# A two-layer decoder trunk: block products of the expert down projection, seven for eight in 38 of 64 steps

## The chip, the cores and the metric

The kernel runs on one core of one Trainium2 chip. The metric is the device time of one execution in microseconds (us). Three runs of the kernel before gave 3980.77, 3981.47 and 3985.25 us; the median is 3981.47.

Names: PE is TensorE (matrix products), PEld its weight loads, DVE is VectorE, ACT ScalarE, POOL GpSimd, SP the queue that issues DMAs. [...] "L356" is line 356 of the kernel file.

## The reference

Two layers. In each, 512 tokens of width 1024 pass a mixer (four parallel heads), then PEER, an expert layer with a product-key choice of 16 of 16384 one-neuron experts for each of 8 heads, then a gated embedding.

```python
def peer(z, w_q, sub_keys, u_tab, v_tab):
    ...
    def block(args):
        zt, et, gt = args
        act = jax.nn.gelu(jnp.einsum('tkd,td->tk', u_tab[et], zt))
        return jnp.einsum('tk,tkd->td', gt * act, v_tab[et])
...
        h = h + peer(rmsnorm(h, ffn_norm[l]), peer_wq[l], peer_subkeys[l], peer_u[l], peer_v[l])
```

The kernel does not gather. It computes the activations of all 16384 experts, multiplies them by a gate that is zero where an expert was not chosen, and multiplies the result (512 x 16384) by V (16384 x 1024).

## The kernel before

The experts are cut into 128 chunks of 128. All products are f32r matrix products of 128 x 128 weights with 512 columns. Each factor is split into a high part (a copy rounded by ACT, L359) and a low part (the difference, on DVE or POOL, L360), and a product is three matrix products: high by high, high by low, low by high (`group3`).

For a chunk the up product is 24 matrix products into one bank `ps_u` (`u_mm`), then ACT's gelu into `dact`. `weigh` multiplies by the gates `dg` on DVE (L341) and splits into `whi`, `wlo`; `split_v` splits the chunk of V into `vhi`, `vlo` (128x1024). The down product works on two chunks at a time: `down(a0, dh)` makes, for one half of the 1024 output columns, four token blocks of 128 tokens; each is six matrix products into a bank `ps_v` and one DVE addition to the residual `h` (L1695).

One pass of the final loop of `gen_dense` (L1735) is one chunk: loads for later chunks, `split_v` and `up` of the chunk two ahead, then four token blocks of `down`. The up products of the first 60 chunks (`NA`) have been made earlier, in `gen_ahead`, beside the choice of the experts and the gates, and went to DRAM (`Ad`); they are loaded again. The up products of the other 68 chunks are made in the loop.

So the expert stage of a layer has two stretches: chunks 0 to 59, in which PE has only down products and DVE all the small work, and chunks 60 to 127, in which up and down products alternate and POOL makes `ulo`. In layer 0 the preparation of the next layer's S5 head (`gen_Cprep`) is mixed in from the 57th pass on (`NP`, `RP`). `gen_Cprep` also runs once at the start, for layer 0.

The order on each engine's queue is fixed when the program is built: a scheduler plays the program through with its own costs and lists each engine's instructions in the order it found. On the chip each engine takes its list in order and waits where a semaphore says so.

## Time and profile before

| what | value |
|---|---|
| median of three runs | 3981.47 us |
| the profiled execution's own time | 3985.38 us |
| its span, first to last instruction | 3983.6 us |
| mean granted TensorE clock | 0.988 |
| PE busy | 3896.2 us, 98% |
| DVE busy | 2903.5 us, 73% |
| ACT busy | 1534.6 us, 39% |
| POOL busy | 551.1 us, 14% |

The busy shares are averages over stages. The expert stage of layer 0 lies between about 860 and 1930 us, that of layer 1 between about 2820 and 3895 us; in the stretches of 50 us that are shown below, the number of matrix products, the granted clock and DVE's busy time are read together.

### The profile page before, as it was taken

What the parts mean: (1) busy time and instruction counts of PE and PEld (TensorE: products, weight loads), DVE (VectorE), ACT (ScalarE), POOL (GpSimd) and SP (SyncE); (2) the same over time, 40 slices, a digit from 0 to 9 for tenths busy, and PEclk for the clock granted to TensorE, in tenths of its full rate; (3) what the DMA queues carried; (4) which work ended last, traced back from release to release, by engine and by line L of the source; (5) the groups of instructions that cost most, each with busy time, mean ns of one, the idle gap of its engine ahead of it and who ended that gap; (6) DMA issues with size and microseconds to landing.
All of it is one profiled execution on the core that took longest, in us unless ns stands there. A gap on an engine that the chain in (4) does not pass through costs nothing.

```text
span 3983.6 us, 54438 instructions
## 1 busy us (share of the span) xinstructions
PE 3896.2 (98%) x20648; PEld 3233.8 (81%) x20648; DVE 2903.5 (73%) x5905; ACT 1534.6 (39%) x2253; POOL 551.1 (14%) x470
## 2 busy tenths in 40 slices
PE   7999999999999999999999899999999999999998
PEld 6878888878888888888898787777788888888887
DVE  9785899968888665555565768998688865555555
ACT  4454255652232332222443443466422232222223
POOL 4321000010002222222031210000100012222220
PEclk9999999999999999999999999999999999999999
DMA  4223254766653433333231232556766533333422
GB/s 146 69 80 103 78 201 175 259 242 196 201 171 132 140 122 132 122 111 122 82 101 55 65 118 94 196 214 238 240 191 201 163 105 133 111 122 108 135 81 90
DMA packets 318215, 562.34 MB, mean 141 GB/s; under 512 B 19200, under 2 KB 207744, under 8 KB 312576
## 3 DMA queue, kind: packets, MB, share of 16 engines
q1 hardware_dynamic: 317952, 558.86, 41.9%
q8 instruction: 162, 2.65, 0.3%
q14 instruction: 101, 0.83, 0.1%
HBM read 443.96 MB, written 114.83 MB: 140 GB/s over the span
## 4 chain that ended last, share of the span: by engine, by line
PE 90%; DVE 6%; DMA 2%; issue 1%; ACT 1%; POOL 1%; SPq 0%; POOLq 0%; DVEq 0%; ACTq 0%
PE ps_u L356 35%; PE ps_v L356 34%; PE ps_j L356 5%; PE ps_g L356 5%; PE ps_d L356 3%; PE ps_r L356 2%; PE ps_q L356 2%; PE ps_s L356 1%; DVE dc L350 0%; DMA wraw<-in_ple_wg_dram 0%; DVE wlo L360 0%; PE ps_t L373 0%; DVE sb L341 0%; PE ps_d L718 0%; DMA s5t<-Td 0%
## 5 line engine op out<-in xcount | busy, mean ns | idle before, releaser
L1695 DVE TENSOR_TENSOR h<-h,ps_v 128x512 f32<-128x512 f32 x1024 | 677.0, 682 | 620.0 <-PE ps_v L356 618.8
L356 PE MATMUL ps_u<-zhi,ulo 128*128 128x512 f32 x2048 | 813.8, 398 | 2.9 <-POOL ulo L360 2.3
L356 PE MATMUL ps_u<-zhi,uhi 128*128 128x512 f32 x2048 | 810.9, 396 | 2.8 <-ACT uhi L359 2.4
L356 PE MATMUL ps_u<-zlo,uhi 128*128 128x512 f32 x2048 | 808.8, 395 | 0.0
L356 PE MATMUL ps_v<-vhi,whi 128*128 128x512 f32 x2048 | 797.6, 390 | 5.1 <-ACT whi L359 5.1
L356 PE MATMUL ps_v<-vlo,whi 128*128 128x512 f32 x2048 | 797.2, 390 | 1.7 <-DVE vlo L360 1.7
L356 PE MATMUL ps_v<-vhi,wlo 128*128 128x512 f32 x2048 | 795.6, 389 | 0.0
L360 POOL TENSOR_TENSOR ulo<-uraw,uhi 128x1024 fp32r<-128x1024 f32 x136 | 331.2, 2436 | 2175.0 <-ACT uhi L359 1573.8
L359 ACT CAST uhi<-uraw 128x1024 fp32r<-128x1024 f32 x256 | 269.7, 1054 | 868.9 <-PE ps_u L356 590.9
L359 ACT CAST whi<-dact 128x512 fp32r<-128x512 f32 (+2 forms) x264 | 159.4, 607 | 788.3 <-issue 368.8
L356 PEld LDWEIGHTS ps_v<-vhi,whi 128*128 128x128 f32 x2048 | 384.7, 188 | 88.2 <-ACT whi L359 6.0
L356 PEld LDWEIGHTS ps_u<-zhi,ulo 128*128 128x128 f32 x2048 | 385.2, 188 | 87.5 <-POOL ulo L360 3.2
L356 PEld LDWEIGHTS ps_u<-zhi,uhi 128*128 128x128 f32 x2048 | 385.3, 188 | 86.5 <-ACT uhi L359 3.7
L356 PEld LDWEIGHTS ps_u<-zlo,uhi 128*128 128x128 f32 x2048 | 385.1, 188 | 83.6
L356 PEld LDWEIGHTS ps_v<-vlo,whi 128*128 128x128 f32 x2048 | 384.6, 188 | 83.6 <-DVE vlo L360 2.5
L356 PEld LDWEIGHTS ps_v<-vhi,wlo 128*128 128x128 f32 x2048 | 384.5, 188 | 81.4
L341 DVE TENSOR_TENSOR dact<-dact,dg 128x512 f32<-128x512 f32 (+2 forms) x264 | 331.9, 1261 | 35.1 <-ACT dact L353 18.7
L360 DVE TENSOR_TENSOR vlo<-vraw,vhi 128x1024 fp32r<-128x1024 f32 x256 | 312.3, 1241 | 28.3 <-ACT vhi L359 28.2
L353 ACT ACTIVATE tstg<-ps_g 128x512 f32<-128x512 f32 x256 | 264.2, 1156 | 128.2 <-PE ps_g L356 126.1
L359 ACT CAST vhi<-vraw 128x1024 fp32r<-128x1024 f32 x256 | 262.2, 1048 | 22.9 <-PE ps_v L356 18.9
L360 DVE TENSOR_TENSOR wlo<-dact,whi 128x512 fp32r<-128x512 f32 (+2 forms) x264 | 177.0, 674 | 37.9 <-ACT whi L359 23.9
L338 DVE TENSOR_TENSOR to<-t_iota,tii 128x1024 f16<-128x1024 bf16 x256 | 172.7, 685 | 1.9 <-ACT tii L353 1.7
(470 smaller groups left out, 5379.8 us busy)
## 6 DMA issues: line engine op xcount, KB each, us to landing
uraw<-in_uT_dram SPq DMA_DIRECT2D x256, 512.0 KB, 3.4
vraw<-in_v_dram SPq DMA_DIRECT2D x256, 512.0 KB, 4.0
Gd<-tstg SPq DMA_DIRECT2D x32, 2048.0 KB, 7.3
dg<-Gd SPq DMA_DIRECT2D x64, 768.0 KB, 5.2
Ad<-aout SPq DMA_DIRECT2D x120, 256.0 KB, 2.2
...
```

The lines of the kernel that those rows point to most:

```text
L338: (eng or self.V).tensor_tensor(out, a, b, op=op)
L341: (eng or self.V).tensor_tensor(out, a, b, op=ALU.mult)
L353: self.A.activation(out, x, f, **k)
L356: self.PE.matmul(out, l, r, start=start, stop=stop)
L359: self.A.copy(hi, x)
L360: (lo_eng or self.V).tensor_tensor(lo, x, hi.bitcast(F32), op=ALU.subtract)
L1695: self.reached = V.tensor_tensor(self.h[:, tb, ds], self.h[:, tb, ds], ps, op=ALU.add).ins
```

## The change

A step is now four chunks, that is two pairs, 32 steps per layer. In a step of the old kind ("eight") every half of V's columns is multiplied as before: 96 matrix products. In a step of the new kind ("seven") the step is a 2 x 2 block product: A has two halves of the tokens (256 each) by two chunk pairs, B has two chunk pairs by two halves of the columns. The four output blocks are made of seven block products (Winograd's form): DVE makes four sums of blocks of A and four of B, and each product is 12 matrix products.

| product | A side | B side | goes to |
|---|---|---|---|
| 1 | A11 | B11 | kept in two PSUM banks over all seven-steps of the layer (`one`) |
| 5 | S1 = A21 + A22 | T1 = B12 - B11 | added to `sums[5]` in SBUF |
| 7 | A11 - A21 | B22 - B12 | added to `sums[7]` |
| 6 | S2 = S1 - A11 | T2 = B22 - T1 | added to `sums[6]` |
| 2 | A12 | B21 | added to `h` |
| 4 | A22 | T2 - B21 | subtracted from `h` |
| 3 | A12 - S2 | B22 | added to `h` |

`combine` adds what `one` and `sums` hold to `h`, once per layer, in its last step. Seven-steps are 15 in layer 0 (from step 11 on, three of four) and 23 in layer 1 (from step 1 on, three of four); step 31 is an eight in both.

The 60 chunks whose up products run ahead are now chunks 0 to 7 and every even chunk from 8 to 110 (`AHEAD`), so that steps 2 to 27 have two up products each and steps 28 to 31 four. `ulo` in the loop is made on DVE (`self.split` without `G`). V and the activations are loaded and split by pairs; loads and bytes are the same. The S5 preparation for the next layer is mixed into steps 1 to 10 of layer 0, all eights. `up` has two PSUM banks for three, so that `one` has two. In `gen_Cprep` four small tiles and `wr` lie in the memory of `CA`, so that its POOL memset comes later.

The removed bodies of `split_u`, `split_v`, `up`, `weigh`, `down` and the loop over `a0` stand in the section on the kernel before. The core of the diff (the helpers that only load are left out):

```diff
@@ gen_Cprep
-        G.memset(self.CA.rearrange("p a b c d -> p (a b c d)"), 0.0)
-        dt, mag, ang, sn, cs = t("sdt"), t("smag"), t("sang"), t("ssn"), t("scs")
+        dt, sn, cs, den = (p[1][:, N * i : N * i + N] for i in range(4))
+        wr = p[1][:, 4 * N : 4 * N + 4 * P].rearrange("p (k n) -> p k n", k=4)
+        mag, ang = t("smag"), t("sang")
...
         save(0)
+        G.memset(self.CA.rearrange("p a b c d -> p (a b c d)"), 0.0)
...
@@ class constants
-    NP = 56
-    NA = 60
+    NP = 7
+    AHEAD = list(range(8)) + list(range(8, 112, 2))
+    NA = len(AHEAD)
+    SEVEN = (11, 1)
+    EIGHT = 4
@@ gen_ahead
-                nc.sync.dma_start(raws[a], self.ap["uT"][l, a])
+                nc.sync.dma_start(raws[a], self.ap["uT"][l, self.AHEAD[a]])
@@ peer
-                bu, bv = banks(pp, "u", 3), banks(pp, "v", 4)
-                gs = [(d, 1)]
+                bu, bv = banks(pp, "u", 2), banks(pp, "v", 4)
+                self.eights_done = False
                 if prep is not None:
-                    kp = self.pool(c1, "pk", so)
                     self.mix([(self.first(d, self.NP), 1)])
-                    gs.append((self.behind(prep(kp, banks(pp, "k", 1))), self.RP))
-                self.mix(gs)
+                    with ExitStack() as c2:
+                        kp = self.pool(c2, "pk", so)
+                        bk = banks(self.pool(c2, "pks", space=PSUM), "k", 1)
+
+                        def eights():
+                            while not self.eights_done:
+                                next(d)
+                                yield
+
+                        e = eights()
+                        self.mix([(self.behind(prep(kp, bk)), self.RP), (e, 1)])
+                        drain((e, 1))
+                sm = self.pool(c1, "sm", so), banks(self.pool(c1, "sms", space=PSUM), "p", 2)
+                self.mix([(d, 1)])
@@ gen_dense
+        NS, S0 = P // 4, self.SEVEN[l]
+        pos = {a: i for i, a in enumerate(self.AHEAD)}
+        later = [a for a in range(P) if a not in pos]
+        acts, vr, gts, us, raws = {}, {}, {}, {}, {}
+        seven = lambda s: S0 <= s < NS - 1 and (s - S0) % self.EIGHT != self.EIGHT - 1
+        sevens = [s for s in range(NS) if seven(s)]
...
+        def split_u(i):
+            if i < len(later):
+                hi = pool.tile([P, KD, P], F32R, name="uhi", tag="uhi", bufs=2)
+                lo = pool.tile([P, KD, P], F32R, name="ulo", tag="ulo", bufs=2)
+                self.split(hi, lo, raws.pop(i))
+                us[i] = hi, lo
+                load_u(i + 2)
...
+        def weigh(a, b0=0, b1=16):
+            t = acts[a // 2][:, a % 2].rearrange("p (b t) -> p b t", b=16)[:, b0:b1]
+            self.mul(t, t, gts[a // 4][:, b0:b1, a % 4, :])
+        def up(i):
+            a = later[i]
+            split_u(i + 1)
+            for _ in self.u_mm(z, bank_u, *us.pop(i), pair(a // 2)[:, a % 2]):
+                pass
+            weigh(a)
+        def parts(kind, n):
+            return [pool.tile([P, 2, n], F32R, name=kind + x, tag=kind + x, bufs=4) for x in ("hi", "lo")]
+        def v_parts(x):
+            p = parts("v", 512)
+            self.split(p[0], p[1], x)
+            return p
...
+        def dot(ps, w, v, t, first=True, last=True):
+            ts = slice(t * P, (t + 1) * P)
+            for k in range(2):
+                self.group3(ps, w[0][:, k, ts], w[1][:, k, ts], v[0][:, k], v[1][:, k], first and k == 0, last and k == 1)
+        def to_h(tb, dh, ps, op=ALU.add):
+            hs = self.h[:, tb, 512 * dh : 512 * dh + 512]
+            self.reached = V.tensor_tensor(hs, hs, ps, op=op).ins
...
+        def sevens_of(s):
+            A = lambda i, j: acts[2 * s + j - 1][:, :, 256 * (i - 1) : 256 * i]
+            B = lambda j, k: vr[2 * s + j - 1][:, :, 512 * (k - 1) : 512 * k]
+            st = lambda: sp.tile([P, 2, 256], F32, name="dsum", tag="dsum", bufs=2)
+            tt = lambda: sp.tile([P, 2, 512], F32, name="dtum", tag="dtum", bufs=2)
+            x, ops = {}, {}
+            def make(p):
+                if p == 1:
+                    w, v = A(1, 1), B(1, 1)
+                elif p == 2:
+                    w, v = A(1, 2), B(2, 1)
+                elif p == 5:
+                    x["s"], x["t"] = w, v = st(), tt()
+                    self.add(w, A(2, 1), A(2, 2))
+                    self.sub(v, B(1, 2), B(1, 1))
+                elif p == 7:
+                    w, v = st(), tt()
+                    self.sub(w, A(1, 1), A(2, 1))
+                    self.sub(v, B(2, 2), B(1, 2))
+                elif p == 6:
+                    w, v = x["s"], x["t"]
+                    self.sub(w, w, A(1, 1))
+                    self.sub(v, B(2, 2), v)
+                elif p == 4:
+                    w, v = A(2, 2), x["t"]
+                    self.sub(v, v, B(2, 1))
+                else:
+                    w, v = x["s"], B(2, 2)
+                    self.sub(w, A(1, 2), w)
+                ops[p] = w_parts(w), v_parts(v)
+            def run(p):
+                w, v = ops.pop(p)
+                for t in range(2):
+                    if p == 1:
+                        dot(one[t], w, v, t, s == sevens[0], s == sevens[-1])
+                        continue
+                    ps = bank_v()
+                    dot(ps, w, v, t)
+                    if p < 5:
+                        to_h(*{2: (t, 0), 3: (t, 1), 4: (2 + t, 0)}[p], ps, ALU.subtract if p == 4 else ALU.add)
+                    elif s == sevens[0]:
+                        self.act(sums[p][:, t], ps, AF.Copy)
+                    else:
+                        self.add(sums[p][:, t], sums[p][:, t], ps)
+            return [(lambda p=p: make(p), lambda p=p: run(p)) for p in (1, 5, 7, 6, 2, 4, 3)]
+        def combine(t):
+            a5, a6, a7 = (sums[p][:, t] for p in (5, 6, 7))
+            to_h(t, 0, one[t])
+            self.add(a6, a6, one[t])
+            self.add(a7, a7, a6)
+            to_h(2 + t, 0, a7)
+            self.add(a6, a6, a5)
+            to_h(t, 1, a6)
+            self.add(a7, a7, a5)
+            to_h(2 + t, 1, a7)
+        slots = lambda s: sevens_of(s) if seven(s) else eights(s)
...
+        for s in range(1, NS):
+            n = len(cur)
+            todo = [a for a in range(4 * s + 4, 4 * s + 8) if a < P and a not in pos]
+            nxt = []
+            for j in range(n):
+                if j == 0:
+                    for a in range(4 * s + 4, min(4 * s + 8, P)):
+                        load_a(a)
+                    load_g(s + 2)
+                    if not sp:
+                        load_v(2 * s + 2)
+                if j == 1:
+                    if sp:
+                        load_v(2 * s + 3)
+                    for a in range(4 * s + 4, min(4 * s + 8, P)):
+                        if a in pos:
+                            weigh(a)
+                if j + 2 == n and s + 1 < NS:
+                    if not sp:
+                        load_v(2 * s + 3)
+                    if s + 1 == S0:
+                        self.eights_done = True
+                        yield
+                        ready(s + 1)
+                    if sp:
+                        load_v(2 * s + 4)
+                    nxt = slots(s + 1)
+                k = j + 2
+                if k < n:
+                    cur[k][0]()
+                elif nxt:
+                    nxt[k - n][0]()
+                for x in range(len(todo)):
+                    if x * (n - 2) // len(todo) == j:
+                        up(i)
+                        i += 1
+                cur[j][1]()
+                if s == NS - 1 and j < 2:
+                    combine(j)
                 yield
+            cur = nxt
```

PE's list of instructions has 20623 rows before and 20180 now, where rows that repeat are drawn together.

Three places in the order of instructions. On DVE, in the middle of the expert stage of layer 0, before (a pass with an up product; `h` is the residual, `dact` the activations, `dg` the gates, `w` and `v` the parts of the two factors):

```order
L1695 TENSOR_TENSOR h_3738<-h_3738,ps_v_15543 128x512
L341 TENSOR_TENSOR dact_15507<-dact_15507,dg_15037 128x512
L1695 TENSOR_TENSOR h_3738<-h_3738,ps_v_15551 128x512
L360 TENSOR_TENSOR wlo_15535<-dact_15507,whi_15534 128x512
L1695 TENSOR_TENSOR h_3738<-h_3738,ps_v_15559 128x512
L1695 TENSOR_TENSOR h_3738<-h_3738,ps_v_15567 128x512
L1695 TENSOR_TENSOR h_3738<-h_3738,ps_v_15619 128x512
L341 TENSOR_TENSOR dact_15583<-dact_15583,dg_15037 128x512
L1695 TENSOR_TENSOR h_3738<-h_3738,ps_v_15627 128x512
L360 TENSOR_TENSOR wlo_15611<-dact_15583,whi_15610 128x512
```

and now, between two seven-steps (`dsum` and `dtum` are the sums of blocks of A and of B, `dsum5` the kept product 5; `ulo` is the up product's low part):

```order
L360 TENSOR_TENSOR wlo_12549<-dsum_12449,whi_12548 128x512
L347 TENSOR_TENSOR dtum_12707<-vraw1_12422 128x1024
L360 TENSOR_TENSOR vlo_12553<-dtum_12450,vhi_12552 128x1024
L347 TENSOR_TENSOR dsum_12449<-dact0_12222,dsum_12449 128x512
L360 TENSOR_TENSOR ulo_12581<-uraw_12327,uhi_12580 128x1024
L341 TENSOR_TENSOR dact1_12477<-dact1_12477,dg_12224 128x512
L347 TENSOR_TENSOR dtum_12450<-dtum_12450,vraw0_12284 128x1024
L360 TENSOR_TENSOR wlo_12573<-dact0_12222,whi_12572 128x512
L344 TENSOR_TENSOR dsum5_12130<-dsum5_12130,ps_v_12556 128x512
L360 TENSOR_TENSOR vlo_12577<-vraw0_12284,vhi_12576 128x1024
L344 TENSOR_TENSOR dsum5_12130<-dsum5_12130,ps_v_12564 128x512
L360 TENSOR_TENSOR wlo_12631<-dact0_12222,whi_12630 128x512
```

The additions to `h` have become fewer; sums, splits of sums and `ulo` stand between them. A split of product 6 (`vlo_12553`) stands ahead of the first addition for product 5 (`dsum5` from `ps_v_12556`), whose bank PE fills two products earlier.

On PE, before, one token block of a `down`, chunk a0 and then a0 + 1 into one bank:

```order
L356 MATMUL ps_v_14222<-vhi_13919,whi_13950 128x512
L356 MATMUL ps_v_14222<-vlo_13920,whi_13950 128x512
L356 MATMUL ps_v_14222<-vhi_13919,wlo_13951 128x512
L356 MATMUL ps_v_14222<-vhi_14007,whi_14038 128x512
L356 MATMUL ps_v_14222<-vlo_14008,whi_14038 128x512
L356 MATMUL ps_v_14222<-vhi_14007,wlo_14039 128x512
```

and now, the end of product 1 into its kept bank (`ps_p`) and the beginning of product 5:

```order
L356 MATMUL ps_p_12129<-vhi_12429,whi_12425 128x512
L356 MATMUL ps_p_12129<-vlo_12430,whi_12425 128x512
L356 MATMUL ps_p_12129<-vhi_12429,wlo_12426 128x512
L356 MATMUL ps_v_12556<-vhi_12457,whi_12453 128x512
L356 MATMUL ps_v_12556<-vlo_12458,whi_12453 128x512
L356 MATMUL ps_v_12556<-vhi_12457,wlo_12454 128x512
```

A bank still takes six matrix products, and the parts have new shapes: the two chunks lie in one tile. On PE a seven-step has 84 of these for 96.

On DVE at the end of layer 1's expert stage, before (the last additions to `h`, and the first splits of the next stage's weights):

```order
L1695 TENSOR_TENSOR h_21618<-h_21618,ps_v_35126 128x512
L360 TENSOR_TENSOR wlo_35285<-wraw_35199,whi_35284 128x1024
L1695 TENSOR_TENSOR h_21618<-h_21618,ps_v_35134 128x512
L360 TENSOR_TENSOR wlo_35291<-wraw_35201,whi_35290 128x1024
L1695 TENSOR_TENSOR h_21618<-h_21618,ps_v_35142 128x512
L1695 TENSOR_TENSOR h_21618<-h_21618,ps_v_35150 128x512
L1695 TENSOR_TENSOR h_21618<-h_21618,ps_v_35158 128x512
L360 TENSOR_TENSOR wlo_35330<-wraw_35288,whi_35329 128x1024
```

and now:

```order
L344 TENSOR_TENSOR dsum6_27384<-dsum6_27384,ps_p_27382 128x512
L1723 TENSOR_TENSOR h_21749<-h_21749,ps_v_35436 128x512
L344 TENSOR_TENSOR dsum7_27385<-dsum7_27385,dsum6_27384 128x512
L1723 TENSOR_TENSOR h_21749<-h_21749,ps_v_35464 128x512
L344 TENSOR_TENSOR dsum7_27385<-dsum7_27385,dsum6_27384 128x512
L1723 TENSOR_TENSOR h_21749<-h_21749,dsum7_27385 128x512
L344 TENSOR_TENSOR dsum6_27384<-dsum6_27384,dsum5_27383 128x512
L1723 TENSOR_TENSOR h_21749<-h_21749,dsum7_27385 128x512
L344 TENSOR_TENSOR dsum6_27384<-dsum6_27384,dsum5_27383 128x512
L1723 TENSOR_TENSOR h_21749<-h_21749,ps_v_35480 128x512
L344 TENSOR_TENSOR dsum7_27385<-dsum7_27385,dsum5_27383 128x512
L1723 TENSOR_TENSOR h_21749<-h_21749,dsum6_27384 128x512
```

The sums of `combine` (`dsum6`, `dsum7`) stand between the last step's additions to `h`.

## Rows read from the trace of the kernel before

**Rows 1.** Page, part 1: busy time of each engine, share of the span, instructions.
```profile
PE 3896.2 (98%) x20648; PEld 3233.8 (81%) x20648; DVE 2903.5 (73%) x5905; ACT 1534.6 (39%) x2253; POOL 551.1 (14%) x470
```

**Rows 2.** Page, part 4: the chain that ended last, by engine and line.
```profile
PE 90%; DVE 6%; DMA 2%; issue 1%; ACT 1%; POOL 1%; SPq 0%; POOLq 0%; DVEq 0%; ACTq 0%
PE ps_u L356 35%; PE ps_v L356 34%; PE ps_j L356 5%; PE ps_g L356 5%; PE ps_d L356 3%; PE ps_r L356 2%; PE ps_q L356 2%; PE ps_s L356 1%; DVE dc L350 0%; DMA wraw<-in_ple_wg_dram 0%; DVE wlo L360 0%; PE ps_t L373 0%; DVE sb L341 0%; PE ps_d L718 0%; DMA s5t<-Td 0%
```

**Rows 3.** Busy time of the engines in stretches: us and instructions, granted clock.
```profile
core 0: us, PE busy (x) PEld busy (x) DVE busy (x) ACT busy (x) POOL busy (x), PEclk, DMA share, GB/s
850.00:900.00 50.00, 44.26 (x187) 34.86 (x185) 28.34 (x43) 20.67 (x29) 10.89 (x4) 0.93 0.79 273
1000.00:1050.00 50.00, 50.00 (x222) 41.39 (x221) 44.26 (x64) 15.21 (x20) 0.00 (x0) 1.00 0.64 196
1200.00:1250.00 50.00, 50.00 (x222) 41.42 (x221) 44.29 (x79) 13.21 (x17) 6.68 (x4) 1.00 0.36 116
1700.00:1750.00 50.00, 50.00 (x223) 41.38 (x222) 28.41 (x33) 15.34 (x20) 11.97 (x5) 1.00 0.31 105
3400.00:3450.00 50.00, 50.00 (x218) 40.63 (x217) 27.32 (x31) 14.51 (x19) 12.03 (x5) 1.00 0.37 121
```

**Rows 4.** Groups on DVE, 900 to 1150 us: count | busy us, mean ns | idle.
```profile
L1695 DVE TENSOR_TENSOR h<-h,ps_v 128x512 f32<-128x512 f32 x178 | 117.5, 682 | 18.7 <-PE ps_v L356 18.5
L360 DVE TENSOR_TENSOR vlo<-vraw,vhi 128x1024 fp32r<-128x1024 f32 x46 | 56.0, 1218 | 0.0
L341 DVE TENSOR_TENSOR dact<-dact,dg 128x512 f32<-128x512 f32 x46 | 32.7, 710 | 1.3 <-DMA dact<-Ad 1.2
L360 DVE TENSOR_TENSOR wlo<-dact,whi 128x512 fp32r<-128x512 f32 x45 | 31.0, 689 | 10.2 <-ACT whi L359 10.2
```

**Rows 5.** DVE in order of time, 1146 to 1150 us: start, duration.
```profile
1146.75 0.68 DVE L360 TENSOR_TENSOR wlo<-dact,whi 128x512 fp32r<-128x512 f32 x1
1147.35 0.68 DVE L1695 TENSOR_TENSOR h<-h,ps_v 128x512 f32<-128x512 f32 x1
1147.95 1.22 DVE L360 TENSOR_TENSOR vlo<-vraw,vhi 128x1024 fp32r<-128x1024 f32 x1
1149.09 0.69 DVE L341 TENSOR_TENSOR dact<-dact,dg 128x512 f32<-128x512 f32 x1
1149.69 0.68 DVE L1695 TENSOR_TENSOR h<-h,ps_v 128x512 f32<-128x512 f32 x1
```

**Rows 6.** Waits of DVE, 900 to 1150 us: total us, times, longest.
```profile
DVE h L1695 <- PE ps_v L356: 18.5, 26, 2.9
DVE wlo L360 <- ACT whi L359: 10.2, 22, 0.5
```

**Rows 7.** Groups on DVE, 500 to 800 us (up products ahead, layer 0).
```profile
L360 DVE TENSOR_TENSOR ulo<-uraw,uhi 128x1024 fp32r<-128x1024 f32 x43 | 52.3, 1216 | 5.0 <-ACT uhi L359 5.0
```

**Rows 8.** Groups on ACT, 1600 to 1850 us.
```profile
L359 ACT CAST uhi<-uraw 128x1024 fp32r<-128x1024 f32 x23 | 24.2, 1053 | 114.9 <-PE ps_u L356 67.7 <-issue 47.2
L359 ACT CAST vhi<-vraw 128x1024 fp32r<-128x1024 f32 x22 | 22.0, 1050 | 2.4 <-PE ps_v L356 2.4
L359 ACT CAST whi<-dact 128x512 fp32r<-128x512 f32 x23 | 14.3, 622 | 59.0 <-DVE dact L341 59.0
L353 ACT ACTIVATE dact<-ps_u 128x512 f32<-128x512 f32 x23 | 13.5, 585 | 0.0
```

**Rows 9.** The gate product on DVE, 1600 to 1850 us.
```profile
L341 DVE TENSOR_TENSOR dact<-dact,dg 128x512 f32<-128x512 f32 x23 | 44.3, 1924 | 0.0
```

**Rows 10.** POOL in the same stretch.
```profile
L360 POOL TENSOR_TENSOR ulo<-uraw,uhi 128x1024 fp32r<-128x1024 f32 x23 | 55.0, 2393 | 195.2 <-ACT uhi L359 195.2
```

**Rows 11.** Waits of PE where the expert stage of layer 0 begins, 840 to 900 us.
```profile
PE ps_v L356 <- ACT whi L359: 2.6, 1, 2.6
PE ps_u L356 <- POOL ulo L360: 1.9, 1, 1.9
```

**Rows 12.** POOL in order of time, 0 to 4 us.
```profile
0.77 2.23 POOL L1112 MEMSET s5p<- 128x2560 f32 x1
```

More of the change, by code (lines that the diff above doesn't have):

```diff
@@ L1679, in weigh @@
[L1679 to L1688 removed]
+                nc.sync.dma_start(o.rearrange("p b a t -> p b (a t)"), g[:, :, 4 * s : 4 * s + 4, :].rearrange("p b a t -> p b (a t)"))
@@ new lines, in v_parts, with w_parts @@
+        def v_parts(x):
+            p = parts("v", 512)
+            self.split(p[0], p[1], x)
+            return p
+        def w_parts(x):
+            p = parts("w", 256)
+            self.split(p[0], p[1], x)
+            return p
+        def dot(ps, w, v, t, first=True, last=True):
+            ts = slice(t * P, (t + 1) * P)
+            for k in range(2):
+                self.group3(ps, w[0][:, k, ts], w[1][:, k, ts], v[0][:, k], v[1][:, k], first and k == 0, last and k == 1)
+        def to_h(tb, dh, ps, op=ALU.add):
+            hs = self.h[:, tb, 512 * dh : 512 * dh + 512]
+            self.reached = V.tensor_tensor(hs, hs, ps, op=op).ins
@@ new lines, in eights, with make, run @@
+        def eights(s):
+            ws, vs = {}, {}
+            def make(q, dh):
+                if dh == 0:
+                    ws[q] = [w_parts(acts[q][:, :, 256 * i : 256 * i + 256]) for i in range(2)]
+                vs[q, dh] = v_parts(vr[q][:, :, 512 * dh : 512 * dh + 512])
+            def run(q, dh):
+                for tb in range(NTB):
+                    ps = bank_v()
+                    dot(ps, ws[q][tb // 2], vs[q, dh], tb % 2)
+                    to_h(tb, dh, ps)
+            return [(lambda q=q, dh=dh: make(q, dh), lambda q=q, dh=dh: run(q, dh)) for q in (2 * s, 2 * s + 1) for dh in range(2)]
@@ new lines, in combine, with ready @@
+        def combine(t):
[9 more added lines that the diff above has]
+        slots = lambda s: sevens_of(s) if seven(s) else eights(s)
+        sp, one, sums = None, None, {}
+        def ready(s):
+            nonlocal sp, one
+            sp, bank_p = spool()
+            one = [bank_p() for _ in range(2)]
+            for p in (5, 6, 7):
+                sums[p] = sp.tile([P, 2, T], F32, name="dsum%d" % p, tag="dsum%d" % p)
+            abuf.insert(0, (lambda: sp, "dact3"))
+            vbuf.insert(0, (lambda: sp, "vraw2"))
@@ new lines, in gen_dense @@
+        load_a(0)
+        load_a(1)
+        load_v(0)
+        yield
+        load_g(0)
+        load_g(1)
+        yield
+        pool = mpool()
+        load_a(2)
+        load_a(3)
+        load_v(1)
+        ws, vs = {}, {}
+        for q in range(2):
+            for a in (2 * q, 2 * q + 1):
+                weigh(a, 0, 12)
+            vs[q, 0] = v_parts(vr[q][:, :, 0:512])
+            h0, h1 = w_parts(acts[q][:, :, 0:256]), parts("w", 256)
+            self.split(h1[0][:, :, 0:P], h1[1][:, :, 0:P], acts[q][:, :, 256 : 256 + P])
+            ws[q] = h0, h1
+            vs[q, 1] = v_parts(vr[q][:, :, 512:D])
@@ L1717, in gen_dense @@
+        load_v(2)
+        load_v(3)
+        load_a(4)
+        load_a(5)
+        for q in range(2):
             for dh in range(2):
-                down(a0, dh, range(3))
+                first(q, dh, range(3))
                 yield
-        for a in range(4):
-            weigh(a, ts[a], 12, 16)
-        load_g(8)
-        for a in range(4, 8):
-            load_u(a)
-            load_v(a)
-        for a0 in (0, 2):
-            for dh in range(2):
-                down(a0, dh, (3,))
-            for a in (a0, a0 + 1):
-                Ws.pop(a)
-                vs.pop(a)
-            split_v(4 + a0 // 2)
-            up(4 + a0 // 2)
-            yield
@@ L1735, in gen_dense @@
-        for a0 in range(4, NC, 2):
-            for part in range(2):
-                n = a0 + 2 + part
-                load_u(n + 2)
-                load_v(n + 2)
-                split_v(n)
-                up(n)
-                split_u(n + 2)
-                down(a0, part)
-                load_g(n + 5)
+        for q in range(2):
+            for a in (2 * q, 2 * q + 1):
+                weigh(a, 12, 16)
+            h1 = ws[q][1]
+            self.split(h1[0][:, :, P:], h1[1][:, :, P:], acts[q][:, :, 256 + P :])
```

139 lines of the change are left out of this document (48 added, 91 removed).

## The prediction

> **What bounds the kernel now.** I read four views, in this order. The first part of the profile's page: PE is busy 98% of the span, DVE 73% [rows 1]. A busy PE could still be waiting inside, so next the chain that ended last: 90% of it is PE, and the up and down products (`ps_u`, `ps_v`) alone are 69% [rows 2]. Third, the same by stretches, since a mean over stages hides what matters here [rows 3]. [...] So there a matrix product that is left out is worth 0.225 us, as long as nothing else becomes the bound. Fourth, who that could be: DVE is busy 44.3 of 50 us where only down products run, and 28.4 where up products run between them. It is close to PE already, and the change gives it more to do. The question is whether DVE has room, and it is answered per step.
>
> The profiled execution took 3985.4 us (span 3983.6 and 1.8 around it), 3.9 above the median. I make the sum against 3985.4 and take 3.9 off at the end. A difference within 0.2%, 8 us, is one that a measurement of this kernel cannot tell from none.
>
> **What PE saves.** A seven-step has 84 matrix products for 96, in 38 steps: 456 x 0.2252 = 102.7 us. Up products are 68 x 24 per layer as before. Layer 1's late stretch makes 218 in 50 us, 0.2294 each [rows 3]; why is not to be seen, so a new placement of the tiles could give either pace: over a layer's 4500 products that is 19 us up or down, which I put into the range and not into the sum.
>
> **What DVE gets.** The durations of single instructions are 0.68 to 0.71 us for 128x512 and 1.22 for 128x1024 [rows 4, 7]. But in order of time one starts 0.60 us after a 128x512 and 1.14 after a 128x1024 [rows 5]: the next begins before the last has ended, and the start-to-start time is what a full queue costs. Sums of blocks do not occur in before; they are f32 additions of the same shapes, from SBUF like the splits, and I give them the splits' times. A seven-step with two up products has on DVE, of 128x512: 4 gate products, 7 `wlo`, 4 sums of A, 12 additions from PSUM, 27 x 0.60 = 16.2 us; of 128x1024: 7 `vlo`, 4 sums of B, 2 `ulo`, 13 x 1.14 = 14.8. Together 31.0. PE needs 84 + 48 = 132 products, 29.7 us. An eight-step has 24 x 0.60 + 6 x 1.14 = 21.2 on DVE against 144 products, 32.4 on PE.
>
> To this come DVE's waits for ACT: 10.2 us beside 91 splits [rows 4, 6], 0.11 per split. The waits for PE in the same rows are no cost, there DVE was early. With 16 splits a seven-step comes to 32.8, an eight-step with 10 to 22.3. In a cycle of three sevens and an eight DVE then needs 3 x 32.8 + 22.3 = 120.7 us and PE 3 x 29.7 + 32.4 = 121.5. It just fits, if the eight's 10 us of room can be used for the 3 x 3.1 = 9.3 us by which DVE falls behind in the sevens. The order of instructions says how far: DVE splits product 6 before it adds up product 5, so PE has two finished products (24 x 0.225 = 5.4 us) and mostly an up product (5.4 us) in its list when DVE starts the next. So 5.4 to 10.8 of the 9.3 us are covered. I take a loss of 2 us in each of 10 cycles, 20 us in all. The bounds: 0 if all is covered, and 32 x 3.1 = 99 if nothing is (32, because 6 of the 38 steps have four up products: 180 products, 40.5 us on PE, more than DVE needs).
>
> What waits behind what: an addition for a product holds DVE until PE has filled the bank, and behind it stand the splits for the product after next, for which PE waits last of all. The gate product waits for ACT's gelu; it belongs to the next step, some 20 us ahead of its use. ACT is not near the bound: 7 x (0.62 + 1.05) + 2 x (1.05 + 0.59) = 15.0 of 29.7 us [rows 8].
>
> [...] In rows 5 instructions overlap by 0.08 us. [...]
>
> **`ulo` on DVE** is in the 31.0. On POOL it took 2.39 us [rows 10], and beside it the gate product took 1.92 for 0.71 us [rows 4, 9]; in seven-steps POOL has nothing to do, so I take the undisturbed 0.60 for it. If the cover were wrong it would cost 4 x 1.3 us of DVE a step.
>
> **The S5 preparation** moves to steps 1 to 10 of layer 0. In before, mixed with up products, DVE was busy 44.3 of 50 us and PE still made 222 in the stretch at 1200 us [rows 3]. Eights leave it 10 us of room each. I take 0, and if the room were not there DVE's part of the preparation would be late: 44.3 - 28.4 = 15.9 us in 50 by the two stretches, and with some three such stretches of it about 48 us.
>
> **The ends.** `combine` is 16 DVE instructions per layer, 9.6 us, in a step whose 96 products take 21.6 us on PE; each stands between two additions that free a bank. A bank is six products, 1.35 us, and an addition with its share of `combine` up to 1.8: 8 x 0.45 = 3.6 us a layer. I take 7 for both (bounds 0 and 19).
>
> **The beginnings.** PE waits 2.6 and 1.9 us where layer 0's expert stage starts [rows 11]; the first loads and splits are the same in number but by pairs. I take 0 (bounds -5 and 5 per layer). At the program's start the memset of 2.23 us [rows 12] moves from an empty POOL to a place behind a save; DVE waits for it there: 1 us (0 to 3).
>
> **Loads** are the same bytes, at 105 to 196 GB/s now [rows 3] and about 150 in a seven-step: no term.
>
> **The sum:** -102.7 + 20 + 7 + 1 = -74.7; 3985.4 - 74.7 = 3910.7; on the scale of the median **3906.8 us**.
>
> **The rivals.**
>
> *DVE sets the pace of every seven-step, and the eights give nothing back.* For it: both queues are taken in order, only four pairs of split tiles exist, and DVE is at 104% to 110% of PE in such a step. Against it: the order lets DVE be two products ahead, and rows 3 show DVE at 89% with no wait of PE. Price: 32 x 1.3 = 42 without waits for ACT and 99 with them, in place of the 20: 3929 to 3986, its middle 3957. Chance 0.22, of which 0.06 lies within 8 us of no change.
>
> *Slower: DVE's instructions do not overlap in the new order.* If each of the 40 instructions holds DVE to its end, a seven-step is 27 x 0.69 + 13 x 1.22 = 34.5 us, and a step alone is then longer than the 32.4 of the eight-step that it replaces. 32 x (34.5 - 29.7) = 154; 3981.5 - 102.7 + 8 + 154 = 4041 us. The change turns from gain to loss where a seven-step takes (102.7 - 8)/32 = 3.0 us more than PE's 29.7, that is at 32.7, only 1.7 above the bare sum. Against it: rows 5 show overlap although these instructions read what ACT and PE have just made. Chance 0.10.
>
> *The change does not save the products.* PE's list is shorter by 443 rows for 456 expected (rows that repeat are drawn together), so it does; no chance of its own.
>
> *All is covered:* 3981.5 - 102.7 + 8 = 3887, with a faster pace in layer 1 down to 3868. This is the lower half of the forecast's own range, 3868 to 3929, and the forecast with it has 0.68.
>
> **The numbers.** Forecast 0.68, DVE's pace 0.22, slower 0.10. The range 3868 to 3965 holds the forecast's and a little over half of the first rival's. Faster by over 0.2%: 0.68 + 0.16 = 0.84. Within: 0.06. Slower: 0.10.
>
> **What would show it.** In stretches of seven-steps in the new profile: PE over 98% busy with 218 to 222 products in 50 us, and DVE at 45 to 50, would show the forecast right; PE at 90 to 95% with waits of `ps_v` on DVE's `vlo` and `wlo` the first rival, and the size is the sum of these waits. A seven-step of 30 to 31 us, from one `ps_p` to the next, is the forecast, 33 the turning point. DVE's starts on sums 0.60 and 1.14 apart would show the row durations right; 0.69 and 1.22 the second rival. A wait of PE in step 31 of over 4 us would show the ends to be dearer. The forecast is wrong if PE's waits in the seven-steps come to more than 60 us.

## The result, and the profile after

The changed kernel took 3879.55 us in the median of four runs (3877.58 to 3882.84), the kernel before 3982.68 beside it: a ratio of 0.9741, 95% interval 0.9725 to 0.9758. That is 103.1 us less. The forecast said 3906.8, range 3868 to 3965: the direction and the range held, and the time came out 27 us below the forecast. The profiled execution took 3877.58 us, span 3875.8.

The first part of the page after, and the first lines of its chain:

```profile
PE 3792.5 (98%) x20192; PEld 3143.2 (81%) x20192; DVE 3264.3 (84%) x6437; ACT 1720.2 (44%) x2489; POOL 219.9 (6%) x334
```

```profile
PE 88%; DVE 8%; DMA 1%; issue 1%; ACT 1%; POOL 1%; SPq 0%; DVEq 0%; POOLq 0%; ACTq 0%
PE ps_u L356 35%; PE ps_v L356 30%; PE ps_j L356 6%; PE ps_g L356 5%; PE ps_d L356 3%; PE ps_p L356 3%; PE ps_r L356 3%; PE ps_q L356 2%; PE ps_s L356 1%; DVE h L1723 1%; DVE wlo L360 1%; DMA s5t<-Td 1%; DVE dc L350 1%; PE ps_t L373 0%; DVE ulo L360 0%
```

Beside [rows 1, 2]: PE is 103.7 us less busy with 456 matrix products fewer (20648 to 20192), DVE 361 us more, POOL 331 less, and the chain is still PE's. Busy time in stretches of the expert stages (columns as in [rows 3]):

```profile
850.00:900.00 50.00, 44.70 (x180) 35.05 (x179) 34.92 (x52) 20.14 (x27) 0.00 (x0) 0.93 0.84 289
1400.00:1450.00 50.00, 50.00 (x223) 41.41 (x222) 46.18 (x62) 19.85 (x26) 0.00 (x0) 1.00 0.56 176
1600.00:1650.00 50.00, 50.00 (x222) 41.41 (x221) 48.81 (x65) 23.73 (x31) 0.00 (x0) 1.00 0.57 184
3100.00:3150.00 50.00, 50.00 (x218) 40.59 (x217) 46.81 (x62) 23.01 (x30) 0.00 (x0) 1.00 0.44 133
3400.00:3450.00 50.00, 50.00 (x218) 40.76 (x217) 42.78 (x56) 16.68 (x22) 0.00 (x0) 1.00 0.55 180
```

In the sevens PE makes as many products in 50 us as before (218 to 223), while DVE goes to 43 to 49. Its groups from 1400 to 1650 us:

```profile
L1723 DVE TENSOR_TENSOR h<-h,ps_v 128x512 f32<-128x512 f32 x70 | 46.6, 680 | 7.0 <-PE ps_v L356 6.8
L360 DVE TENSOR_TENSOR vlo<-dtum,vhi 128x1024 fp32r<-128x1024 f32 x25 | 30.4, 1218 | 1.1 <-ACT vhi L359 0.8
L341 DVE TENSOR_TENSOR dact<-dact,dg 128x512 f32<-128x512 f32 x34 | 23.2, 683 | 0.6 <-DMA dact<-Ad 0.6
L360 DVE TENSOR_TENSOR ulo<-uraw,uhi 128x1024 fp32r<-128x1024 f32 x17 | 20.7, 1220 | 2.4 <-ACT uhi L359 2.2
L347 DVE TENSOR_TENSOR dtum<-vraw,vraw 128x1024 f32<-128x1024 f32 x6 | 7.3, 1221 | 0.1
L344 DVE TENSOR_TENSOR dsum<-dact,dact 128x512 f32<-128x512 f32 x6 | 4.1, 683 | 0.0
```

The sums of blocks (`dtum`, `dsum`) take what the splits of their shapes take, 1221 and 683 ns for 1218 (`vlo`) and 682 (`wlo`), and the gate product is at 683 where it was 1924 beside POOL [rows 9]. In order of time the starts are 0.60 and 1.14 apart, as in [rows 5], for sums too:

```profile
1511.08 0.68 DVE L360 TENSOR_TENSOR wlo<-dsum,whi 128x512 fp32r<-128x512 f32 x1
1511.68 0.68 DVE L344 TENSOR_TENSOR dsum<-dsum,ps_v 128x512 f32<-128x512 f32 x1
1512.28 1.22 DVE L360 TENSOR_TENSOR vlo<-vraw,vhi 128x1024 fp32r<-128x1024 f32 x1
1513.41 0.68 DVE L344 TENSOR_TENSOR dsum<-dact,dact 128x512 f32<-128x512 f32 x1
1514.01 0.68 DVE L344 TENSOR_TENSOR dsum<-dsum,ps_v 128x512 f32<-128x512 f32 x1
```

One whole cycle of three sevens and an eight, from the first product of one `ps_p` (1397.40 us) to that of the fourth step on, the same columns as the stretches; and DVE's waits in it (total, times, longest):

```profile
1397.40:1519.80 122.40, 122.40 (x542) 101.41 (x541) 116.20 (x151) 51.80 (x67) 0.00 (x0) 1.00 0.49 158
```

```profile
DVE h L1723 <- PE ps_v L356: 3.7, 6, 1.7
DVE dsum L344 <- PE ps_v L356: 0.8, 1, 0.8
DVE ulo L360 <- ACT uhi L359: 0.7, 1, 0.7
DVE vlo L360 <- ACT vhi L359: 0.4, 1, 0.4
DVE dact L341 <- DMA dact<-Ad: 0.4, 1, 0.4
```

The cycle is PE's: 122.40 us of 122.40 for its 540 products, 0.2267 each. The prediction had 121.5, by 50/222; but the 222 of a stretch count products that only reach into it, too. DVE is busy 116.2 and waits 6.0, of which 1.1 for ACT and 4.5 for PE, where it is early. From 900 to 1845 us in layer 0, and from 2820 to 3770 in layer 1, PE waits for nobody. Its waits where layer 0's stage begins, 840 to 900 us, and at the ends of the two stages (1845 to 1910 and 3770 to 3876 us):

```profile
PE ps_v L356 <- ACT whi L359: 2.7, 1, 2.7
PE ps_v L356 <- DVE h L1723: 2.0, 1, 2.0
PE ps_v L356 <- DVE vlo L360: 0.5, 1, 0.5
...
PE ps_v L356 <- DVE h L1723: 1.2, 1, 1.2
...
PE ps_v L356 <- DVE h L1723: 1.4, 3, 0.7
PE ps_g L356 <- DVE h L1723: 1.1, 1, 1.1
```

Of the signs that the prediction named, PE's full stretches, DVE's starts and the short waits at the ends are there. Single seven-steps with two up products, from one `ps_p` to the next, took 25.8 to 34.0 us in layer 0, as neighbouring steps interleave differently each time; only the mean over cycles, 122.4 us, can be compared.

### The profile page after: what moved, and what is told of

Its sections match the earlier page's. It is cut to its first block, busy times and chain, and to the rows that moved or that the text cites. A ratio compares the mean times of both kernels' runs of the same rounds, so it can differ in the third digit from the quotient of the medians.

```text
span 3875.8 us, 54231 instructions
## 1 busy us (share of the span) xinstructions
PE 3792.5 (98%) x20192; PEld 3143.2 (81%) x20192; DVE 3264.3 (84%) x6437; ACT 1720.2 (44%) x2489; POOL 219.9 (6%) x334
## 4 chain that ended last, share of the span: by engine, by line
PE 88%; DVE 8%; DMA 1%; issue 1%; ACT 1%; POOL 1%; SPq 0%; DVEq 0%; POOLq 0%; ACTq 0%
PE ps_u L356 35%; PE ps_v L356 30%; PE ps_j L356 6%; PE ps_g L356 5%; PE ps_d L356 3%; PE ps_p L356 3%; PE ps_r L356 3%; PE ps_q L356 2%; PE ps_s L356 1%; DVE h L1723 1%; DVE wlo L360 1%; DMA s5t<-Td 1%; DVE dc L350 1%; PE ps_t L373 0%; DVE ulo L360 0%
## 5 line engine op out<-in xcount | busy, mean ns | idle before, releaser
L356 PE MATMUL ps_v<-vhi,whi 128*128 128x512 f32 x1744 | 683.6, 392 | 12.9 <-DVE h L1723 7.5
L356 PE MATMUL ps_v<-vlo,whi 128*128 128x512 f32 x1744 | 683.4, 392 | 0.5 <-DVE vlo L360 0.5
L356 PE MATMUL ps_v<-vhi,wlo 128*128 128x512 f32 x1744 | 682.3, 392 | 0.0
L1723 DVE TENSOR_TENSOR h<-h,ps_v 128x512 f32<-128x512 f32 x644 | 429.6, 681 | 88.3 <-PE ps_v L356 85.6
L356 PEld LDWEIGHTS ps_v<-vhi,whi 128*128 128x128 f32 x1744 | 328.8, 189 | 88.2 <-DVE h L1723 9.7
L360 DVE TENSOR_TENSOR ulo<-uraw,uhi 128x1024 fp32r<-128x1024 f32 x256 | 311.3, 1216 | 104.0 <-ACT uhi L359 103.1
L353 ACT ACTIVATE tstg<-ps_g 128x512 f32<-128x512 f32 x256 | 264.1, 1155 | 127.9 <-PE ps_g L356 125.5
L359 ACT CAST whi<-dact 128x512 fp32r<-128x512 f32 (+1 forms) x222 | 136.0, 614 | 379.1 <-PE ps_v L356 289.2
L360 DVE TENSOR_TENSOR vlo<-vraw,vhi 128x1024 fp32r<-128x1024 f32 x218 | 265.3, 1218 | 34.3 <-ACT vhi L359 32.4
L359 ACT CAST whi<-dsum 128x512 fp32r<-128x512 f32 x152 | 94.3, 622 | 323.9 <-PE ps_v L356 179.7
L341 DVE TENSOR_TENSOR dact<-dact,dg 128x512 f32<-128x512 f32 (+2 forms) x264 | 175.0, 670 | 57.4 <-DMA dact<-Ad 36.3
L359 ACT CAST vhi<-dtum 128x1024 fp32r<-128x1024 f32 x152 | 159.3, 1048 | 92.3 <-PE ps_v L356 79.4
```

The lines of the kernel that those rows point to most:

```text
L341: (eng or self.V).tensor_tensor(out, a, b, op=ALU.mult)
L353: self.A.activation(out, x, f, **k)
L356: self.PE.matmul(out, l, r, start=start, stop=stop)
L359: self.A.copy(hi, x)
L360: (lo_eng or self.V).tensor_tensor(lo, x, hi.bitcast(F32), op=ALU.subtract)
L1723: self.reached = V.tensor_tensor(hs, hs, ps, op=op).ins
```

## The experiments

The theory: the saved products are worth PE's pace, and as long as the sum of DVE's queue over a cycle fits under PE's, nothing is lost. The rivals: each seven-step in which DVE is longer than PE costs something by itself; or the gain has another source (the order by pairs, POOL's absence).

**Eights only.** Everything of the change but the seven-steps.

```diff
-        seven = lambda s: S0 <= s < NS - 1 and (s - S0) % self.EIGHT != self.EIGHT - 1
+        seven = lambda s: False
...
-                if s == NS - 1 and j < 2:
-                    combine(j)
```

> All 64 steps are eights, the rest of the changed kernel stays: every other chunk ahead, ulo on DVE, pairs, the S5 preparation early. Theory (the gain is the 456 products that PE does not make, and the rest is neutral): 3879.6 + 102.7, less some 4 us for the sums at the ends, 3978 us. Rival (a good part of the gain comes from the new interleaving and from POOL being quiet): 3930 to 3960 us.

Measured: 3980.78 us (3976.02 to 3988.37), ratio to before 1.0001 (0.9992 to 1.0011). So the order by pairs, the new chunks ahead, the S5 preparation beside eights and `ulo` on DVE come to nothing together (within some 4 us), and the sevens with `combine` are worth 3980.8 - 3879.6 = 101.2 us of the 102.7 that their products cost. By the two traces, from a stage's first `ps_v` to its last, it is 40.0 us in layer 0 and 57.4 in layer 1, 97.4 together (each stage within some 2 us, by a repeat below): so 1.5 to 5.3 us are lost, the larger part in layer 1. PE's waits at the beginning are in this kernel too (2.7 and 2.0 us), so they do not come from the sevens. DVE has room in it:

```profile
1400.00:1450.00 50.00, 50.00 (x222) 41.39 (x222) 34.49 (x47) 15.22 (x19) 0.00 (x0) 1.00 0.45 145
```

**All sevens.** No eight between them, 50 seven-steps.

```diff
-    EIGHT = 4
+    EIGHT = 64
```

> No eights between: 50 seven-steps, 12 more. PE makes 144 products fewer, 32 us. Theory (DVE has 31.0 us of work in a seven-step with two up products against 29.7 on PE, and lookahead covers some 10 us per layer once): 42 such steps fall behind by 1.3 us each, 55, less 20 covered: 3879.6 - 32.4 + 35 = 3882 us, with PE waiting for DVE's splits some 35 us. Rival A (DVE is no bound at all): 3847 us. Rival B (DVE waits for ACT 0.11 us per split as predicted, 32.8 us a step): 3940 to 3960 us.

Measured: 3864.47 us (3862.97 to 3869.84), ratio 0.9709 (0.9693 to 0.9725). Twelve sevens more should save 12 x 12 x 0.2252 = 32.4 us; 15.1 are left of it, so 17 are lost, half of the theory's 35. The direction is the theory's, the size not. Three steps without eights, from `ps_p` to `ps_p`, and PE's waits from 2820 to 3780 us:

```profile
1501.60:1593.81 92.21, 90.16 (x397) 73.98 (x396) 92.21 (x120) 41.33 (x54) 0.00 (x0) 1.00 0.46 152
```

```profile
PE ps_u L356 <- ACT dact L353: 8.2, 8, 1.0
```

Here DVE is never idle. It starts 119 of the three steps' 120 instructions in 92.21 us, which comes to 31.0 us for a seven-step, as worked out from start-to-start times in the prediction. PE's wait reads "ACT dact", the gelu that reads a `ps_u` bank; but ACT is busy 41 of 92 us. Eleven times in the two layers (three times in layer 0) PE waits 1.0 us for a gelu. Each of these gelus starts right behind a `whi` on ACT's list, and ten of those `whi` had just waited until PE was through with a `ps_v` product. So these waits go through the order of ACT's list; that the full DVE is what stands behind them is the theory, and no single wait shows it.

By the stages of the traces layer 0 became 7.5 us shorter than in the change, for 60 products that are worth 13.5, and layer 1 11.1, for 84 worth 19.3: both lose, 6.0 and 8.2 us. The theory's 35 us took 29.7 us of PE for a seven-step in both layers. By the starts of its products it is 29.9 in layer 0 (0.2267 each) and 30.5 in layer 1 (0.2312, 3000 to 3700 us of the change's trace). DVE's 31.0 is then longer by 1.1 and 0.5 us, 16 x 1.1 + 26 x 0.5 = 31 us for the 55, of which the theory has 20 covered: 11 are left. Measured are 14 to 17, so that 3 to 6 us stay open.

**An eight after every six sevens.** `EIGHT = 7`, 44 seven-steps.

> An eight after every six sevens, 44 seven-steps for 38. Theory (DVE needs 6 x 31.0 + 21.2 = 207.2 us in seven steps, PE 6 x 29.7 + 32.4 = 210.6, so DVE keeps up on the mean and lookahead has to cover 8 us): 72 products fewer, 3879.6 - 16.2 = 3863 us. Rival (the eights must give back after every third step, cover is used up): no change or slower, 3880 to 3895 us.

Measured: 3870.19 us (3864.77 to 3871.35), ratio 0.9717 (0.97 to 0.9733): 9.4 us below the change, between the 16 of the theory and none. By the stages of the traces, again from the first `ps_v` to the last, layer 0 became 6.2 us shorter (8.1 expected) and layer 1 9.1 (8.3), 15.3 together, and PE waits for nobody in the middle of either. So the trace is with the theory: six sevens to an eight are still covered. What is missing in the total lies between the two stages, where these kernels are alike: 895.4 us here for 889.7 in the change, and 886 to 895 over the changed kernels of this document. A difference of a few us in a total is therefore not to be read as one of the sevens.

**More work for DVE.** Sums of blocks of B are made again, with the same result: one (e4), two (e11) or four (e5) additions of 128x1024 more in every seven-step. The form with four:

```diff
                     self.sub(v, B(1, 2), B(1, 1))
+                    self.sub(v, B(1, 2), B(1, 1))
+                    self.sub(v, B(1, 2), B(1, 1))
...
                     self.sub(v, B(2, 2), B(1, 2))
+                    self.sub(v, B(2, 2), B(1, 2))
+                    self.sub(v, B(2, 2), B(1, 2))
```

One more:

> One of a seven-step's sums of blocks of B is made twice: 32.1 us of VectorE's queue per seven-step and 3 x 32.1 + 21.2 = 117.6 per cycle against 121.5. Theory (an eight gives back what three sevens lack): no loss, 3880 +- 3 us. Rival (each seven-step over TensorE's time costs part of its excess): the excess grows by 1.14 us in 32 steps, so 36 us if all of it is lost and some 3890 to 3900 if a third is.

Two more:

> Two of a seven-step's sums of blocks of B are made twice, which adds two additions of 128x1024 on VectorE: 31.0 + 2 x 1.14 = 33.3 us of its queue per seven-step, and 3 x 33.3 + 21.2 = 121.1 us per cycle of three sevens and an eight, against 121.5 on TensorE in layer 0 and 123.8 at layer 1's slower pace. This is the load that the prediction supposed (120.7), and for which it took a loss of 2 us per cycle. Theory: what the prediction mis-sized was VectorE's load, and the eights give back what the sevens lack as long as the cycle's sum fits; then the loss at this load is small: layer 1 keeps 2.7 us of room per cycle and loses 0 to 5 us in all, layer 0 has 0.4 and loses 0 to 8 in all, 3880 to 3892 us. Rival: the cover is bounded by how far VectorE's list runs ahead of TensorE's, and at 10 us of deficit per cycle some of it is lost, 2 us or more in each of 10 cycles: 3900 us or above.

Four more:

> In each seven-step two of the sums of B are made three times over instead of once: 4 more DVE instructions of 128x1024, 4.56 us, the results unchanged. Theory (a cycle of three sevens and an eight has 121.5 - 114.2 = 7.3 us of room on DVE, 2.4 per seven-step): 3 x 4.56 = 13.7 is 6.4 over the room in each of 10 cycles, 3879.6 + 64 = 3944 us, PE waiting for DVE's splits. Rival (DVE far from a bound): 3880 us. Rival (no payback by the eights, DVE already at the edge in each seven-step): 32 x 4.56 = 146, 4020 us.

Measured: one, 3883.31 us (3880.82 to 3885.86), ratio 0.9759 (0.9743 to 0.9775); two, 3888.48 (3885.91 to 3890.7), 0.9768 (0.9751 to 0.9784); four, 3914.86 (3906.2 to 3918.73), 0.9835 (0.9819 to 0.9851). Against the change: 3.8, 8.9 and 35.3 us. The intervals of the ratios leave some 9 us either way, so one cannot be told from none, and two hardly; in the trace with two, PE waits 1.2 and 2.6 us in the middle of the stages, where the change has no wait. Two is as the theory had it, and one nearly (0.3 us outside it); the rivals' 3890 and 3900 fell. The 32 seven-steps with two up products grew by 36 and 73 us of DVE together, and all but 3.8 and 8.9 of it disappeared. With four the cycle no longer fits (3 x 35.6 + 21.2 = 128 us, against 122.4 and, at 0.2312, 124.8), and the loss sets in: in the middle of layer 1 the cycles take 127.9 to 128.6 us. The theory's 64 us again took 121.5 for both layers; with these paces it is some 44 (4 cycles of 5.6 us and 6.7 of 3.2), and why only 35 were measured stays open. Stretches with two, in which both engines are full:

```profile
3100.00:3150.00 50.00, 50.00 (x218) 40.64 (x217) 50.00 (x65) 22.14 (x28) 0.00 (x0) 1.00 0.37 125
3400.00:3450.00 50.00, 50.00 (x219) 40.74 (x218) 50.00 (x64) 22.99 (x29) 0.00 (x0) 1.00 0.59 192
```

and PE's two longest waits with four, 2820 to 3780 us:

```profile
PE ps_u L356 <- ACT dact L353: 13.2, 12, 1.9
PE ps_v L356 <- DVE vlo L360: 2.1, 2, 1.2
```

**One product ahead for two.** The sums and splits are written one product ahead of its matrix products.

```diff
-            cur[q][0]()
+            if q == 0:
+                cur[q][0]()
...
-                k = j + 2
+                k = j + 1
```

> The changed kernel with the operands of a product made one product ahead instead of two (the order of the list; tiles are the same). Theory (over a cycle DVE has room, but in the three sevens it falls back 3.9 us, and one finished product with or without an up product covers 2.7 to 8.1): a loss of 0 to 1.2 us in each of 10 cycles, 3880 to 3892 us. Rival (the lookahead is what makes the change work at all): 3.1 us and more in each of 32 steps, above 3930 us. Rival (the lookahead does nothing): 3879 us, within 4.

Measured: 3879.81 us (3877.34 to 3881.96), ratio 0.9745 (0.9729 to 0.9761), the time of the change. It decides nothing: the scheduler made the same order from it. By lines and names, DVE's 6437 instructions come in the same order in both traces but for four near the end of layer 1's stage, and ACT's 2489 in the same throughout. What a shorter lead would cost stays open. As a repeat of the change it shows what chance does to a trace: its span is 4.4 us longer (3880.2), and its stages are by 2.1 and 1.8.

**`ulo` on POOL again**, with the change's eights (e10) and with all sevens (e7).

```diff
-                self.split(hi, lo, raws.pop(i))
+                self.split(hi, lo, raws.pop(i), G)
```

> 50 seven-steps as in the run without eights between, and ulo in the expert loop on POOL. There DVE was busy 50.0 of 50 us, so what leaves DVE must show. Theory (beside POOL's 2.4 us DVE's own instructions take some 1.2 us longer, as the gate product did in the kernel before, 1.92 for 0.71 us; so 1.14 us saved and 1.2 lost per ulo): 3864 us within 8, DVE still busy 50 of 50. Rival (DVE is relieved by 2.3 us per step): PE sets the pace, 3850 us.

> The changed kernel with its eights, and ulo in the expert loop on POOL as in the kernel before. Without eights that cost 48 us, because an instruction of DVE beside POOL's 2.5 to 2.9 us takes 1.6 us longer and only 1.14 is saved: 0.46 us more per ulo. Theory (what counts is the sum of a cycle): 3 x 31.9 + 22.1 = 117.8 us of DVE against 121.5 of PE, still room: 3880 us, within 8. Rival (each longer instruction holds PE up, whatever the sum): 3900 to 3925 us.

Measured: with all sevens 3912.62 us (3907.4 to 3915.57), ratio 0.9828 (0.9811 to 0.9844), 48 above the same without POOL; both expectations fell. With eights 3910.61 (3899.35 to 3915.8), ratio 0.9824 (0.9803 to 0.9845), 31 above the change, as the rival had it. DVE's groups of the latter, 1400 to 1650 us:

```profile
L1723 DVE TENSOR_TENSOR h<-h,ps_v 128x512 f32<-128x512 f32 x68 | 44.2, 675 | 3.7 <-PE ps_v L356 3.7
L360 DVE TENSOR_TENSOR vlo<-vraw,vhi 128x1024 fp32r<-128x1024 f32 x26 | 34.7, 1336 | 0.0
L341 DVE TENSOR_TENSOR dact<-dact,dg 128x512 f32<-128x512 f32 x30 | 34.0, 1138 | 6.7 <-DMA dact<-Ad 5.1 <-issue 1.3 <-DVE vlo L360 0.2
L360 DVE TENSOR_TENSOR wlo<-dact,whi 128x512 fp32r<-128x512 f32 x26 | 24.1, 927 | 0.0
L347 DVE TENSOR_TENSOR dtum<-vraw,vraw 128x1024 f32<-128x1024 f32 x6 | 11.5, 1915 | 0.1
```

The additions from PSUM are as short as ever (675 ns for 680). So are most sums and splits of blocks, with both inputs in SBUF (`vlo` from `dtum` 1211 for 1218, `wlo` from `dsum` 678 for 682). The other four groups shown, also with both inputs in SBUF, became longer: 26 x 0.12 + 30 x 0.46 + 26 x 0.25 + 6 x 0.69 = 27.6 us for 16 `ulo`, 1.7 each, where DVE itself would have spent 1.14. The order of time shows how (DVE, then POOL):

```profile
1510.27 0.67 DVE L360 TENSOR_TENSOR wlo<-dact,whi 128x512 fp32r<-128x512 f32 x1
1510.87 1.21 DVE L347 TENSOR_TENSOR dtum<-dtum,vraw 128x1024 f32<-128x1024 f32 x1
1512.01 0.67 DVE L344 TENSOR_TENSOR dsum<-dsum,ps_v 128x512 f32<-128x512 f32 x1
1512.61 2.83 DVE L360 TENSOR_TENSOR vlo<-vraw,vhi 128x1024 fp32r<-128x1024 f32 x1
1515.37 0.68 DVE L344 TENSOR_TENSOR dsum<-dsum,ps_v 128x512 f32<-128x512 f32 x1
```

```profile
1506.22 8.14 POOL L360 TENSOR_TENSOR ulo<-uraw,uhi 128x1024 fp32r<-128x1024 f32 x1 [16.38 <-ACT uhi L359]
```

POOL's split lies there 8.14 us (spans on POOL are rough) for the 2.4 of [rows 10], from 1506.22, beside seven DVE instructions with two inputs in SBUF (1506.19 to 1512.01), each as long as without it (0.67 or 1.2 us). It ends at 1514.36, 2.35 us after the next DVE instruction, an addition from PSUM, began (1512.01); and the `vlo` behind that addition takes 2.83 us for 1.22 and ends 1.08 after POOL's end. So in this place first POOL's instruction is the longer one and then DVE's. The mean of the 26 such `vlo` went from 1216 to 1336 ns. By what mechanism the two make each other longer was not shown.

Why 31 us are lost though DVE's sum over the cycle (about 119: 114.2 + 8 x 0.56) still fits, the trace shows for the most part. The two expert stages are 17.0 and 13.4 us longer than the change's. PE's waits in the middle of the two (900 to 1850 and 2860 to 3780 us) come to 11.2 and 9.8 us, where the change has none. Those of the first:

```profile
PE ps_v L356 <- DVE dsum L344: 5.8, 4, 1.8
PE ps_v L356 <- DVE h L1723: 4.0, 4, 3.0
PE ps_k L356 <- DVE s5p L1190: 1.4, 1, 1.4
```

Nearly all are for additions that free a bank, and what stands in front of these on DVE's list is of two kinds. In four waits (9.0 us in the two layers) it is an instruction of 2.9 to 3.4 us beside POOL's split. In six (9.8 us) it is a gate product that waits for its load, as here (DVE, then the load's issue and PE):

```profile
1423.35 2.30 DVE L360 TENSOR_TENSOR wlo<-dact,whi 128x512 fp32r<-128x512 f32 x1
...
1428.39 0.69 DVE L341 TENSOR_TENSOR dact<-dact,dg 128x512 f32<-128x512 f32 x1 [1.61 <-DMA dact<-Ad]
1429.00 0.68 DVE L344 TENSOR_TENSOR dsum<-dsum,ps_v 128x512 f32<-128x512 f32 x1
1425.67 0.33 SPq L1660 DMA_DIRECT2D dact<-Ad  x1
1429.82 0.47 PE L356 MATMUL ps_v<-vhi,whi 128*128 128x512 f32 x1 [1.76 <-DVE dsum L344]
```

POOL's split begins at 1422.69, and the `wlo` beside it lasts 2.30 us for 0.68. The load of the next activations, which waits for a tile that a `wlo` reads, is issued as this one ends (1425.67) and lands 2.6 us later. DVE comes to the gate product before that, stands idle for 1.61 us, and the addition behind it comes too late for PE. So one instruction that became longer also moves a load, and the sum of DVE's busy time has no term for that. Measured by the starts of PE's products, which also shows delays too short to leave PE idle, the same stretches lose 13.4 and 14.2 us, so that some 3 of the 31 stay open.

**More sevens.** All sevens, in layer 0 from step 8 on, with the S5 preparation mixed in faster so that it ends before: 53 seven-steps.

```diff
-    RP = 0.5
+    RP = 0.8
...
-    SEVEN = (11, 1)
-    EIGHT = 4
+    SEVEN = (8, 1)
+    EIGHT = 64
```

> All seven-steps, in layer 0 from step 8 on instead of 11 (53 in all), with the S5 preparation mixed in at 0.8 for 0.5 so that it still ends before. Theory: 36 more products fewer than with 50, 8.1 us, of which DVE's 1.3 us in each of three steps is given back: 3864.5 - 4 = 3860 us. Rival (the denser preparation fills DVE's room in the eights and PE waits): 3865 to 3875 us.

Measured: 3858.14 us (3857.45 to 3862.52), ratio 0.9692 (0.9676 to 0.9708): the fastest here, 21.4 us below the change. The theory's 3860 held, and the rival fell. A seven that costs DVE 31.0 us is still shorter than the eight's 144 products on PE (32.6), whatever DVE's deficit.

## Why the prediction was right, and where not

*What PE saves*: right. The 0.2252 is 50 us by the 222 products that PE makes in layer 0's full stretches of [rows 3]. 456 products fewer, each worth its pace; 101.2 of 102.7 us by the eights-only kernel. The pace itself was 0.7% too short (0.2267 for 0.2252 by the starts in layer 0). The pace of layer 1's late stretch stayed at 218 in 50 us and is unexplained as before.

*What DVE gets*: right in its bare durations. A cycle was put at 114.2 us and DVE was busy 116.2; a full queue showed 31.0 per seven-step, as put.

*The term that was mis-sized* is "I take a loss of 2 us in each of 10 cycles, 20 us in all". For it and `combine` together the runs show 102.7 - 101.2 = 1.5 us (the intervals of the two ratios leave some 8 us either way; the stages of the traces say 5.3), and PE has no wait in the sevens of either layer. Three things were off. First DVE's load: the 0.11 us of waiting for ACT per split came from a stretch in which DVE also waited 18.5 us for PE, that is, ran out of work [rows 6]. In the new cycle it is 1.1 us for 58 splits where 6.4 were taken, and in the three steps shown of the kernel with all sevens, where DVE has the most to do, it waits for nobody: 92.21 us busy of 92.21. Second the cover: at the load that was taken (120.7; the kernel with two additions has 121.1) the loss was 8.9 us and not 20. Third PE's side of the cycle, 122.4 us for 121.5, and some 125 in layer 1, which gave DVE more room than was counted. So the mechanism, eights giving back what sevens lack, was the right one and its price too high.

*The ends*: 7 was taken, and PE's waits beside `combine` come to 1.2 and 2.5 us. *The beginnings*, taken at 0: the first `ps_v` of layer 0 starts 3.4 us earlier than before (856.4 for 859.8), but among the changed kernels it starts anywhere from 856.3 to 860.6, so that this is no gain of the change. From 840 to 900 us the waits are 5.2 us for 5.8 ([rows 11] has the two longest of these, 4.5). *The memset* at the start was taken at 1: in the first 140 us of the trace DVE does not wait for it. *The S5 preparation* cost nothing, as said: eights only has the time of before.

With 20 and 7 put at 0 and 3, the prediction's own sum gives 3906.8 - 24 = 3883; the 3 us to the measured time are as much as single runs of the changed kernel differ from their median.

*The rivals.* DVE pacing each seven-step (3929 to 3986): fell, there is no wait of PE for `vlo` or `wlo` in the sevens. Once eights are left out, something of it shows, 14 to 17 us in 42 such steps, where its least, 1.3 us a step, would be 55: PE's own steps are longer than 29.7 us, above all in layer 1, and part is covered. The slower one (4041): fell, the starts are 0.60 and 1.14 us apart for sums as for splits, and on a full queue a seven-step took 31.0 us and not 34.5. "All is covered" (3887), counted as the lower half of the forecast's own range, is what happened.

*`ulo` on DVE* was right, and for the reason given, that DVE's instructions beside POOL's split become longer. The prediction saw it on the gate product alone (4 x 1.3 us a step); the runs show it on splits and sums too (means of 1336 ns for 1216 and 927 for 682 of splits, 1915 for 1221 of sums), and 31 us for the whole.
